# Seven-product units: partial sums kept in PSUM, two units interleaved, some GpSimd work given to VectorE

## The chip, the cores and the metric

The kernel runs on one core of one Trainium2 chip. The metric is the device time of one execution in microseconds. The core's engines run side by side, each through its own list of instructions in order: TensorE (PE; its weight loads are shown as PEld), VectorE (DVE), ScalarE (ACT), GpSimd (POOL), and SyncE (SP), whose queue issues all DMA transfers. The engines wait for each other through semaphores. Matrix products land in PSUM, eight banks of 512 fp32 per partition; GpSimd is not used on PSUM here. Everything else lies in SBUF or in DRAM.

## The reference

One layer of a hybrid backbone on 1024 latent tokens and 256 context tokens, D_MODEL = 1024, fp32:

```python
h   = modulate(rmsnorm(x, norm1_w), shift1, scale1)
z, f, uv, gate, ... = split(h @ w_in)            # IN_COLS columns, gate: 3 * 1024
m   = sigmoid(g0) * (y_ssd @ w_ssd_o) + sigmoid(g1) * (y_fft @ w_fft_o) + sigmoid(g2) * (y_gmlp @ w_gmlp_o)
x   = x + gate1 * (m @ w_out)
h2  = modulate(rmsnorm(x, norm2_w), shift2, scale2)
a, v = split(dwconv3(h2 @ ffn_w_up))             # 2 * 2816 columns, conv along rows of 64 tokens
x   = x + gate2 * ((silu(a) * v) @ ffn_w_down)
out = rmsnorm(x, final_norm_w)
```

y_ssd is a bidirectional state-space scan, y_fft a two-dimensional Fourier mixing, y_gmlp a spatial gating.

## The kernel before

Activations lie with channels on partitions and the 1024 tokens along the free axis, in tiles of 128 x 1024. Each fp32 factor is split in two parts (a high part rounded by ScalarE's copy, and the rest, a subtraction on VectorE or GpSimd), and each product is three matmuls: high x high, high x low, low x high.

The large products use a seven-product form on 2 x 2 blocks. A *unit* computes two output tiles of 128 channels (r = 0, 1) for two token halves of 512 (h = 0, 1): four quarters. With weight blocks A11, A12, A21, A22 the weights are A11 (1), A12 (2), S2 = A21 + A22 - A11 (6), S1 = A21 + A22 (5), S3 = A11 - A21 (7), A12 - S2 (3) and A22 (4); the activation operands B1 to B7 are built once per stage. With products P1 to P7 the quarters are

```
(0,0) = P1 + P2            (0,1) = P1 + P6 + P5 + P3
(1,0) = P1 + P6 + P7 + P4  (1,1) = P1 + P6 + P7 + P5
```

`unit_steps` (line 820) runs one unit. `raw` (824) loads the four weight blocks, `s_` (829) forms the sums on VectorE, `put` (834) splits a weight into a tile of `wpool` (6 buffers): the high part on ScalarE (836), the low part on GpSimd (837). `prod` (840) issues the matmuls of one product, 3 x kh (843 to 845). P1 + P2 goes to bank X, P6 + P7 + P4 to bank Y, P5 + P3 to bank Z; X and Y come from four rotating banks, Z from two. ScalarE copies P1 out of X (856). `add` (849) forms each of the other three quarters in SBUF tiles r0 and r1 from bank Y, the copy p1 and bank Z, in five VectorE additions per unit; then `consume` gets each quarter. Between P6 and P7, and between P7 and P4, Y has to be read by VectorE.

The stages with such units, in order:

- gates (`gate_unit`, 1050): 12 units, kh = 4. `consume` is a sigmoid on ScalarE into r0 or r1 (1052), stored to Sg. After each addition of most units a step of `modulation` (1066) runs on VectorE as side work: two products with a running sum, L1078.
- SSD merge (1113): 4 units, kh = 4. `consume` multiplies by the loaded gate on VectorE (1117). The operand is built by `build` (786), mostly on VectorE, while the last gate units run.
- up projection (`up_unit`, 1316): 22 units, kh = 4. `consume` is a convolution of width 3 over tokens: a ScalarE activation (1306) and two VectorE instructions (1308, 1310), all reading the quarter; for r = 0 a tanh (1328, ScalarE) and a VectorE product (1329); after each of (0,1) and (1,0) a GpSimd product with the gated half (1331). After every second unit four VectorE sums (1353 to 1356) form the operands of the down stage and are stored to Gd. The first two units start early, amid the second norm.
- down projection (1364): the inner dimension in chunks of 6, 6, 4 and 4 tiles (the last 2 tiles are done plainly). A chunk loads its operand parts from Gd and splits them (166, 167), then runs 4 units, kh = 3 or 2. `consume` adds the quarter, scaled by the gate g2, onto the tile xf in SBUF (1386). xf comes from Xs and takes the two buffers that the gate tiles gt of the up stage used.
- the fourth chunk by token halves (`unit_by_halves`, 931), with the last products and the final norm between its halves (1446).

The order of the instructions on each engine is made before the run by a planner that simulates the engines; `tc.high_priority` moves instructions ahead in it (PRE for the weights, CRIT for the additions).

```python
        prod(Y, 6, True)
        add(c12, Y, p1, True)
        prod(Z, 5, True)
        prod(Y, 7, False)
        add(c22, Y, p1, True)
        add(c22, Z, c22, True)
        consume(1, 1, c22, R)
```

Of the kernel before, what the change touches and what calls it, by code (L numbers as in the profile page):

```python
# [32 lines left out]
def hybrid_block_kernel(ctx: ExitStack, tc: tile.TileContext, a, dbg=None):  # L33
# [158 lines left out]
    # ------------------------------------------------ first norm and its modulation  # L192
# [100 lines left out]
    # dt and the decays that follow from it, tokens on partitions  # L293
# [45 lines left out]
    # ------------------------------------------------ step sizes; context pass for the initial states  # L339
# [66 lines left out]
    # ------------------------------------------------ xBC and the chunked scan  # L406
# [214 lines left out]
    # ------------------------------------------------ z gate, group norm, gMLP branch  # L621
# [57 lines left out]
    # ------------------------------------------------ Fourier branch: both transforms  # L679
# [43 lines left out]
    # ------------------------------------------------ gMLP branch  # L723
# [29 lines left out]
    # ------------------------------------------------ seven-product form of the large products  # L753
# [66 lines left out]
    def unit_steps(src0, src1, kh, B, consume, nm, side=None, early=None):  # L820
        n = kh * P
        w = {}
# [11 lines left out]
        def put(p, ap):  # L834
            t = wpool.tile([P, 2, n], F32R, tag="w", name=f"w{p}{nm}")
            S.activation(t[:, 0, :], ap, AF.Copy)  # L836
            G.tensor_tensor(t[:, 1, :], ap, f32(t)[:, 0, :], op=ALU.subtract)  # L837
            w[p] = t.rearrange("p q (k c) -> p q k c", c=P)

        def prod(o, p, first):  # L840
            for k in range(kh):
                xh, xl_ = B[p][k]
                PE.matmul(o, w[p][:, 0, k, :], xh, start=first and k == 0, stop=False, skip_group_check=not first)  # L843
                PE.matmul(o, w[p][:, 0, k, :], xl_, start=False, stop=False, skip_group_check=not first)
                PE.matmul(o, w[p][:, 1, k, :], xh, start=False, stop=k == kh - 1, skip_group_check=not first)

        def add(o, x, y, hook=False):
            with tc.high_priority(offset=CRIT):
                ins = V.tensor_tensor(o, x, y, op=ALU.add)  # L849
            if hook and side is not None:  # L850
                with tc.issue_after(ins.ins):
                    next(side, None)

        def copy_p1():
            with tc.high_priority(offset=CRIT):
                S.activation(p1, X, AF.Copy)
# [3 lines left out]
        if early:  # L860
            with tc.high_priority(offset=PRE):
                put(1, raw(11, 0, 0))
                put(2, raw(12, 0, 1))
            prod(X, 1, True)
            copy_p1()
            yield
            prod(X, 2, False)
            yield
            with tc.high_priority(offset=PRE):
                a11, a21 = raw(11, 0, 0), raw(21, 1, 0)  # L870
                a22, a12 = raw(22, 1, 1), raw(12, 0, 1)
                s1_ = s_(1, a21, a22, ALU.add)
                s2_ = s_(2, s1_, a11, ALU.subtract)
                put(3, s_(4, a12, s2_, ALU.subtract))
            W = ps_small("w" + nm, early[0])
            prod(W, 3, True)
            yield
            with tc.high_priority(offset=PRE):
                put(6, s2_)
                put(5, s1_)  # L880
                put(7, s_(3, a11, a21, ALU.subtract))
                put(4, a22)
            yield
        else:
            with tc.high_priority(offset=PRE):
                a11, a21 = raw(11, 0, 0), raw(21, 1, 0)
                a22, a12 = raw(22, 1, 1), raw(12, 0, 1)
                put(1, a11)
                s1_ = s_(1, a21, a22, ALU.add)
                s2_ = s_(2, s1_, a11, ALU.subtract)  # L890
                put(6, s2_)
                put(5, s1_)
                s3_ = s_(3, a11, a21, ALU.subtract)
                put(7, s3_)
                put(2, a12)
                s_(4, a12, s2_, ALU.subtract, s2_)
                put(3, s2_)
                put(4, a22)

        Y = ps4("Y" + nm)  # L900
        Z = ps_small("z" + nm, early[1] if early else ("c", "c2")[un[0] % 2])
        un[0] += 1
        r0 = tpool.tile([P, L], F32, tag="acc", name="r0" + nm)
        r1 = tpool.tile([P, L], F32, tag="acc", name="r1" + nm)
        R = (r0, r1)
        c12, c21, c22 = r0[:, HB:L], r1[:, 0:HB], r1[:, HB:L]
        if early:
            consume(0, 0, X, R)
        else:
            prod(X, 1, True)  # L910
            copy_p1()
        prod(Y, 6, True)
        add(c12, Y, p1, True)
        prod(Z, 5, True)
        prod(Y, 7, False)
        add(c22, Y, p1, True)
        add(c22, Z, c22, True)
        consume(1, 1, c22, R)
        if not early:
# [526 lines left out]
    for u in tail:  # L1446
        next(u)
# [116 lines left out]
```

## Time and profile before

| | |
|---|---|
| time, median of 3 runs | 1992.35 us (1987.56 to 1993.89) |
| profiled execution: span from first to last instruction | 1985.5 us |
| profiled execution: its own time | not listed; the runs lie 2 to 8 us above the span |
| TensorE busy | 1782.9 us, 90% of the span |
| VectorE busy | 1506.0 us, 76% |
| GpSimd busy | 1049.2 us, 53% |
| ScalarE busy | 821.3 us, 41% |

Times are in microseconds from the start of the span, mean durations in the view of groups of instructions in nanoseconds. A line of the profile names the source line, the engine, the operation and its tiles as out<-in (buffer numbers are left out: `up` in a name is the up stage, `g` the gates, `p` the SSD merge, `d` the down stage). Matmuls are pipelined: one is shown with about 0.39 us, but the next starts after about 0.23; so their spacing is read from the starts. A few matmul records may be missing. "idle before <- X" is the time for which an engine stood before an instruction, and what ended it. PEclk is the granted TensorE clock as a share of full speed.

### The profile page before, as it was taken

To read this page: it belongs to the slowest core of one execution; us is meant where nothing else is said; L and a number is where in the kernel's file an instruction comes from. 1 tells how busy PE (TensorE), PEld (TensorE's weight loads), DVE (VectorE), ACT (ScalarE), POOL (GpSimd) and SP (SyncE) were. 2 spreads that over 40 slices of the span, in tenths; PEclk is the share of its full clock that TensorE was granted. 3 is DMA by queue.
4 is the path that set the end of the run, shared out by engine and by line. 5 is a ranking of instruction groups with operands and counts; after the bars stand their busy time and mean duration, and the time that the engine had idled before them with its cause. 6 is when DMAs were issued, how large, how long until landed. Compare 5 with 4: busy or idle time off the path is not lost. (4 is left out here: it accounts for less than half of the span.)

```text
span 1985.5 us, 23581 instructions
## 1 busy us (share of the span) xinstructions
PE 1782.9 (90%) x8148; PEld 1414.7 (71%) x8148; DVE 1506.0 (76%) x1976; ACT 821.3 (41%) x1416; POOL 1049.2 (53%) x707
## 2 busy tenths in 40 slices
PE   4899989888997999998899998898989898889888
PEld 3688766666676888786677886676777776667667
DVE  6876576786676757878786458988888888978896
ACT  5444345554532433334232344343344344434433
POOL 3222265466444655554458555655555565755664
PEclk9999999999998999999999998899999999899998
DMA  8022446554542136662354631132222224643422
GB/s 319 11 67 75 141 151 169 143 171 128 159 142 83 66 110 217 218 218 90 106 182 162 225 132 58 70 105 80 85 85 96 80 85 145 219 145 120 149 88 85
DMA packets 139423, 257.21 MB, mean 130 GB/s; under 512 B 14876, under 2 KB 55708, under 8 KB 137896
## 3 DMA queue, kind: packets, MB, share of 16 engines
q1 hardware_dynamic: 139304, 255.71, 39.1%
q8 instruction: 64, 1.05, 0.2%
q14 instruction: 55, 0.45, 0.1%
HBM read 202.56 MB, written 53.10 MB: 129 GB/s over the span
## 5 line engine op out<-in xcount | busy, mean ns | idle before, releaser
L1078 DVE CUSTOM_DVE_ANT_0 ctanh<-ctanh,crow 128x512 f32<-128x512 f32 x64 | 71.7, 1139 | 24.6 <-DMA ctanh<-in_wmod_dram 24.4
L286 DVE SCALAR_TENSOR_TENSOR acc<-psx,convw,acc 128x1023 f32<-128x1023 f32 (+1 forms) x48 | 61.3, 1277 | 22.9 <-ACT acc L282 22.4
L1331 POOL TENSOR_TENSOR gt<-gt,aa 128x512 f32<-128x512 f32 x44 | 60.1, 1367 | 33.3 <-DVE gt L1310 26.6
L1126 POOL TENSOR_TENSOR pwo<-rwo,pwo 128x512 fp32r<-128x512 f32 x32 | 47.4, 1488 | 48.8 <-ACT pwo L1125 43.4
L555 DVE SCALAR_TENSOR_TENSOR rf<-rs,ncuml,rf 128x128 f32<-128x128 f32 x128 | 47.3, 416 | 31.5 <-ACT rf L554 29.1
L561 POOL TENSOR_TENSOR rf<-rf,G 128x512 f32<-128x512 f32 x32 | 46.0, 1441 | 45.0 <-DVE G L558 34.7
L843 PE MATMUL Yup<-bhh,w4up 128*128 128x512 f32 x88 | 40.9, 464 | 25.8 <-DVE r1up L849 25.8
L558 DVE SCALAR_TENSOR_TENSOR G<-cbm,dtl,G 128x128 f32<-128x128 f32 x128 | 58.6, 516 | 5.5 <-ACT G L557 5.5
L1328 ACT ACTIVATE ft<-aa 128x512 f32<-128x512 f32 x44 | 27.8, 631 | 82.9 <-DVE aa L1310 82.9
L1306 ACT ACTIVATE gt<-r1up,fconvb,fconvw 128x512 f32<-128x512 f32 x44 | 35.8, 814 | 54.2 <-DVE r1up L849 53.6
L837 POOL TENSOR_TENSOR w6up<-S2up,w6up 128x512 fp32r<-128x512 f32 x22 | 35.3, 1603 | 42.2 <-ACT w6up L836 42.2
L554 ACT ACTIVATE rf<-rf,ncuml 128x128 f32<-128x128 f32 x128 | 41.1, 390 | 31.5 <-DMA rf<-Rd 31.5
L1308 DVE SCALAR_TENSOR_TENSOR gt<-r1up,fconvw,gt 128x504 f32<-128x504 f32 x44 | 43.3, 985 | 9.9 <-ACT gt L1306 9.7
L837 POOL TENSOR_TENSOR w5up<-S1up,w5up 128x512 fp32r<-128x512 f32 x22 | 30.4, 1382 | 37.9 <-ACT w5up L836 34.2
L157 PE MATMUL pso<-mh,pwo 128*128 128x512 f32 x128 | 50.2, 392 | 0.0
L153 PE MATMUL pso<-mh,pwo 128*128 128x512 f32 x128 | 49.8, 390 | 0.0
L155 PE MATMUL pso<-ml,pwo 128*128 128x512 f32 x128 | 49.8, 389 | 0.0
L837 POOL TENSOR_TENSOR w2up<-A12up,w2up 128x512 fp32r<-128x512 f32 x22 | 32.1, 1459 | 33.5 <-ACT w2up L836 33.5
L1310 DVE SCALAR_TENSOR_TENSOR gt<-r1up,fconvw,gt 128x504 f32<-128x504 f32 x44 | 48.0, 1092 | 0.4
L510 DVE TENSOR_TENSOR scr<-po,ro 128x512 f32<-128x512 f32 x32 | 21.8, 683 | 34.9 <-ACT ro L497 34.6
L1329 DVE SCALAR_TENSOR_TENSOR aa<-ft,aa 128x512 f32<-128x512 f32 x44 | 46.1, 1047 | 2.7 <-ACT ft L1328 2.7
L520 PE MATMUL pS<-scr,Bt 128*128 128x512 f32 x56 | 32.5, 665 | 15.6 <-DVE scr L510 15.2
(1116 smaller groups left out, 6836.1 us busy)
## 6 DMA issues: line engine op xcount, KB each, us to landing
gr<-Gd SPq DMA_DIRECT2D x70, 256.0 KB, 4.5
ctanh<-in_wmod_dram SPq DMA_DIRECT2D x64, 256.0 KB, 3.1
Gd<-gt SPq DMA_DIRECT2D x10, 1536.0 KB, 6.1
wm<-in_wmod_dram SPq DMA_DIRECT2D x16, 512.0 KB, 9.8
ro<-Rd SPq DMA_DIRECT2D x64, 128.0 KB, 3.3
rf<-Rd SPq DMA_DIRECT2D x32, 256.0 KB, 4.7
rs<-Rd SPq DMA_DIRECT2D x32, 256.0 KB, 3.4
sg<-Sg SPq DMA_DIRECT2D x16, 512.0 KB, 3.6
```

The costliest lines, as they stand in the source:

```text
L153: PE.matmul(o, wh[:, k, :], xh[:, sl], start=st, stop=False)
L155: PE.matmul(o, wh[:, k, :], xl[:, sl], start=False, stop=False)
L157: last_op["mm"] = PE.matmul(o, wl[:, k, :], xh[:, sl], start=False, stop=sp)
L286: V.scalar_tensor_tensor(acc[:, lo:hi], ps[:, lo + o:hi + o], cw[:, t, j:j + 1], acc[:, lo:hi], op0=ALU.mult, op1=ALU.add)
L555: V.scalar_tensor_tensor(E[:, h, :], rs[:, h, :], ncum[:, c, 16 + f:17 + f], E[:, h, :], op0=ALU.add, op1=ALU.min)
L558: V.scalar_tensor_tensor(Gm[:, h, :], cbm[:, 1, :], dtl[:, c, 16 + f:17 + f], Gm[:, h, :], op0=ALU.mult, op1=ALU.add)
L837: G.tensor_tensor(t[:, 1, :], ap, f32(t)[:, 0, :], op=ALU.subtract)
L1078: V.tensor_tensor_reduce(out=wm[:, i], in0=wm[:, i], in1=cr[:, HS[i]], scale=0.5, scalar=0.0, op0=ALU.mult, op1=ALU.add, accum_out=mod2[:, ...
L1126: G.tensor_tensor(t[:, 1, :], raw, f32(t)[:, 0, :], op=ALU.subtract)
L1310: V.scalar_tensor_tensor(a3[:, :, 0:63], p3[:, :, 1:64], fcw[:, t, 2:3], a3[:, :, 0:63], op0=ALU.mult, op1=ALU.add)
L1329: V.scalar_tensor_tensor(ac, th, 1.0, ac, op0=ALU.add, op1=ALU.mult)
L1331: G.tensor_tensor(gt[:, 2 * q + h, :], gt[:, 2 * q + h, :], aa[:, HS[h]], op=ALU.mult)
```

## The change

- The partial sums stay in PSUM. P1, P6, P7 and P4 accumulate one after the other in bank Y, P5 and P3 in Z, P2 alone in X. ScalarE copies Y out after P1 (p1), after P6 (u2) and after P7 (u3). VectorE makes three additions per unit: X + p1 in place in PSUM, Z + u3 into SBUF, Z + u2 in place in PSUM. The quarter (1,0) is bank Y itself. So three of the four quarters reach `consume` in PSUM.
- Units are cut into three steps, and `run_units` interleaves two of them: the first product of the next unit (and the preparation of its weights) comes ahead of P4 and P3 of the current one.
- Gates: the sigmoid writes into p1, u2 or u3, and each half row is stored by itself.
- Up stage: the gate product (1331 before) and the low parts of weights 2 and 3 go from GpSimd to VectorE. The sums of a pair and their stores are issued after the last step of its second unit, that is behind the first product of the next unit.
- Down stage: `sum_steps` has no additions. After each product `consume` adds the bank as it stands onto xf, seven times per unit; the low parts of weights 3 and 4 go to VectorE. The token-half units do the same and their steps are staggered over the four units.
- The first two up units keep their order; their additions go to one tile U, the last one in place in PSUM.

The diff, cut to its core:

```diff
-            G.tensor_tensor(t[:, 1, :], ap, f32(t)[:, 0, :], op=ALU.subtract)
+            (V if p in on_v else G).tensor_tensor(t[:, 1, :], ap, f32(t)[:, 0, :], op=ALU.subtract)
...
+    def unit_steps(src0, src1, kh, B, consume, nm, side=None, on_v=()):
+        w = seven_weights(src0, src1, kh, nm, on_v)
...
+        prod(Y, w[1], B[1], kh, True)
+        keep(p1, Y)
+        yield
...
+        prod(Z, w[5], B[5], kh, True)
+        prod(Y, w[6], B[6], kh, False)
+        keep(u2, Y)
+        prod(X, w[2], B[2], kh, True)
+        add(X, X, p1)
+        consume(0, 0, X, p1)
+        prod(Y, w[7], B[7], kh, False)
+        keep(u3, Y)
+        add(u3, Z, u3)
+        consume(1, 1, u3, u3)
+        yield
+        prod(Y, w[4], B[4], kh, False)
+        consume(1, 0, Y, p1)
+        prod(Z, w[3], B[3], kh, False)
+        add(Z, Z, u2)
+        consume(0, 1, Z, u2)
+        yield
...
+    def sum_steps(src0, src1, kh, B, consume, nm, on_v=()):
...
+        prod(Y, w[1], B[1], kh, True)
+        out(0, 0, Y)
+        yield
...
+        prod(Z, w[5], B[5], kh, True)
+        out(1, 1, Z)
+        prod(Y, w[6], B[6], kh, False)
+        out(0, 1, Y)
+        prod(X, w[2], B[2], kh, True)
+        out(0, 0, X)
+        prod(Y, w[7], B[7], kh, False)
+        out(1, 1, Y)
+        yield
+        prod(Z, w[3], B[3], kh, False)
+        out(0, 1, Z)
+        prod(Y, w[4], B[4], kh, False)
+        out(1, 0, Y)
+        yield
+
+    def run_units(units):
+        units = iter(units)
+        cur = next(units)
+        next(cur)
+        while cur is not None:
+            next(cur)
+            nxt = next(units, None)
+            if nxt is not None:
+                next(nxt)
+            next(cur)
+            cur = nxt
...
-        def consume(r, h, src, R):
-            S.activation(R[r][:, HS[h]], src, AF.Sigmoid)
-            if r != h:
-                SY.dma_start(Sg[b][d + 4 * r], R[r])
+        def consume(r, h, src, spare):
+            S.activation(spare, src, AF.Sigmoid)
+            SY.dma_start(Sg[b][d + 4 * r][:, HS[h]], spare)
...
-                G.tensor_tensor(gt[:, 2 * q + h, :], gt[:, 2 * q + h, :], aa[:, HS[h]], op=ALU.mult)
+                V.tensor_tensor(gt[:, 2 * q + h, :], gt[:, 2 * q + h, :], aa[:, HS[h]], op=ALU.mult)
+        args = (a["wup"][j], a["wup"][NFF + j], 4, B2, consume, f"up{j}")
+        return early_steps(*args, early) if early else unit_steps(*args, on_v=(2, 3))
...
+            return (sum_by_halves if halves else sum_steps)(*args, on_v=(3, 4))
```

## Rows read from the trace of the kernel before

**Rows 1.** Busy times in four stretches: us, then each engine, PEclk, DMA share, GB/s.
```profile
753.28:890.45 137.17, 135.48 (x590) 109.53 (x588) 109.72 (x176) 48.16 (x85) 74.64 (x50) 1.00 0.65 217
890.45:1012.00 121.55, 105.71 (x433) 83.22 (x431) 91.70 (x101) 43.23 (x66) 57.37 (x37) 0.96 0.33 111
1315.32:1670.60 355.28, 323.38 (x1345) 254.75 (x1344) 297.43 (x337) 139.79 (x224) 205.32 (x144) 0.96 0.25 89
1716.00:1957.00 241.00, 214.97 (x886) 170.14 (x885) 206.21 (x252) 95.12 (x169) 148.44 (x122) 0.94 0.38 121
```
In each stretch the engines stand in the order PE, PEld, DVE, ACT, POOL.

**Rows 2.** TensorE's timeline: first matmul of a product and of the next.
```profile
1315.32 0.39 PE L843 MATMUL Xup<-bhh,w1up 128*128 128x512 f32 x1
...
1318.04 0.39 PE L843 MATMUL Yup<-bhh,w6up 128*128 128x512 f32 x1
```

**Rows 3.** Waits from 1250 to 1690 us: total, times, longest.
```profile
ACT aa L1306 <- POOL gt L1331: 57.5, 20, 4.0
...
PEld Yup L843 <- DVE r1up L849: 31.4, 18, 5.5
```

**Rows 4.** TensorE's timeline at its longest stop in the up stage.
```profile
1377.33 0.80 PE L843 MATMUL Yup<-bhh,w4up 128*128 128x512 f32 x1 [5.04 <-DVE r1up L849]
1377.92 0.63 PE L844 MATMUL Yup<-blh,w4up 128*128 128x512 f32 x1
1378.35 0.63 PE L845 MATMUL Yup<-bhh,w4up 128*128 128x512 f32 x1
```

**Rows 5.** Timeline of all engines: a VectorE and a GpSimd instruction that meet.
```profile
1411.44 1.67 POOL L837 TENSOR_TENSOR w7up<-S3up,w7up 128x512 fp32r<-128x512 f32 x1 [0.69 <-ACT w7up L836]
...
1411.99 1.66 DVE L1310 SCALAR_TENSOR_TENSOR aa<-r0up,fconvw,aa 128x504 f32<-128x504 f32 x1
```

**Rows 6.** Single lines (min/median/max ns), then groups of 1315.32 to 1670.60 us.
```profile
L849 DVE TENSOR_TENSOR r1up<-Yup,p1up x44: 672/680/691, 1249.8 to 1714.6; 128x512 f32<-128x512 f32 x44
...
L831 DVE TENSOR_TENSOR S2up<-S1up,A11up x22: 676/680/1785, 1190.7 to 1658.8; 128x512 f32<-128x512 f32 x22
...
L1310 DVE SCALAR_TENSOR_TENSOR gt<-r1up,fconvw,gt 128x504 f32<-128x504 f32 x33 | 35.0, 1059 | 0.3
L1308 DVE SCALAR_TENSOR_TENSOR gt<-r1up,fconvw,gt 128x504 f32<-128x504 f32 x32 | 31.8, 995 | 7.2 <-ACT gt L1306 7.1
...
L831 DVE TENSOR_TENSOR S2up<-A12up,S2up 128x512 f32<-128x512 f32 x16 | 19.7, 1232 | 4.7 <-POOL w6up L837 4.7
L1310 DVE SCALAR_TENSOR_TENSOR aa<-r0up,fconvw,aa 128x504 f32<-128x504 f32 x16 | 19.1, 1193 | 0.3
...
L831 DVE TENSOR_TENSOR S1up<-A21up,A22up 128x512 f32<-128x512 f32 x16 | 16.1, 1008 | 0.0
...
L1308 DVE SCALAR_TENSOR_TENSOR aa<-Xup,fconvw,aa 128x504 f32<-128x504 f32 x16 | 11.7, 734 | 0.5
...
L1331 POOL TENSOR_TENSOR gt<-gt,aa 128x512 f32<-128x512 f32 x32 | 41.2, 1288 | 25.4 <-DVE gt L1310 22.9 <-DVE aa L1329 2.5
...
L856 ACT ACTIVATE p1up<-Xup 128x512 f32<-128x512 f32 x16 | 9.2, 578 | 0.0
```

**Rows 7.** TensorE's timeline near the gates' end; a wait of 680 to 915 us.
```profile
911.66 0.80 PE L843 MATMUL Yg<-hh,w4g 128*128 128x512 f32 x1 [5.72 <-DVE r1g L849]
...
ACT r0g L1052 <- DMA Sg<-r1g: 9.0, 5, 4.3
```

**Rows 8.** Down stage: groups of 1716 to 1957 us, then two timeline rows.
```profile
L1386 DVE SCALAR_TENSOR_TENSOR xf<-r1d,g,xf 128x512 f32<-128x512 f32 x24 | 27.7, 1157 | 2.7 <-DMA xf<-Xs 2.3
...
L1386 DVE SCALAR_TENSOR_TENSOR xf<-Xd,g,xf 128x512 f32<-128x512 f32 x16 | 11.8, 740 | 1.2 <-PE Xd L845 1.2
...
L831 DVE TENSOR_TENSOR S1d<-A21d,A22d 128x384 f32<-128x384 f32 (+1 forms) x10 | 6.7, 670 | 0.0
...
1715.85 0.39 PE L843 MATMUL zd<-gh,w5d 128*128 128x512 f32 x1
...
1743.86 1.28 DVE L1386 SCALAR_TENSOR_TENSOR xf<-r1d,g,xf 128x512 f32<-128x512 f32 x1 [2.28 <-DMA xf<-Xs]
```

More of the change, by code (lines that the diff above doesn't have):

```diff
@@ L836, in put @@
             S.activation(t[:, 0, :], ap, AF.Copy)
-            G.tensor_tensor(t[:, 1, :], ap, f32(t)[:, 0, :], op=ALU.subtract)
[L838 to L845, printed above, removed]
@@ L847, in add, with prod @@
-        def add(o, x, y, hook=False):
+            (V if p in on_v else G).tensor_tensor(t[:, 1, :], ap, f32(t)[:, 0, :], op=ALU.subtract)
+            return t.rearrange("p q (k c) -> p q k c", c=P)
+        return raw, s_, put
+    def prod(o, w, Bp, kh, first):
+        for k in range(kh):
+            xh, xl_ = Bp[k]
+            PE.matmul(o, w[:, 0, k, :], xh, start=first and k == 0, stop=False, skip_group_check=not first)
+            PE.matmul(o, w[:, 0, k, :], xl_, start=False, stop=False, skip_group_check=not first)
+            last_op["PE2"] = PE.matmul(o, w[:, 1, k, :], xh, start=False, stop=k == kh - 1,
+                                       skip_group_check=not first)
@@ L848, in add, with keep @@
+    def unit_steps(src0, src1, kh, B, consume, nm, side=None, on_v=()):
+        w = seven_weights(src0, src1, kh, nm, on_v)
+        def keep(dst, ps):
+            with tc.high_priority(offset=CRIT):
+                S.activation(dst, ps, AF.Copy)
+        def add(o, x, y):
             with tc.high_priority(offset=CRIT):
                 ins = V.tensor_tensor(o, x, y, op=ALU.add)
-            if hook and side is not None:
+            if side is not None:
                 with tc.issue_after(ins.ins):
@@ L900, in unit_steps @@
[L900 to L913, printed above, removed]
@@ L1000, in unit_by_halves @@
         un[0] += 1
[L1001 to L1004 removed]
+        prod(Z, w5, B[5], kh, True)
+        out(1, 1, Z)
         yield
[L1007 to L1009 removed]
+        prod(Z, w3, B[3], kh, False)
+        out(0, 1, Z)
+        yield
     Bh = {p: [] for p in ORDER}
@@ L1358, in hybrid_block_kernel, with gate_tile, up_stage, with_sums @@
         SY.dma_start(Gd[jp][:, 2:8, :], gt[:, 2:8, :])
+    def gate_tile(jp):
+        gts[jp] = mpool.tile([P, 8, HB], F32, tag="m", name=f"gt{jp}")
+    gate_tile(0)
+    for u in pre:
+        for _ in u:
+            pass
+    gate_sums(0)
+    def up_stage():
+        for j in range(2, NFF):
+            if j % 2 == 0:
+                gate_tile(j // 2)
+            yield up_unit(j)
+    def with_sums(units):
+        for j, u in enumerate(units, 2):
+            def steps(j=j, u=u):
+                for n_, _ in enumerate(u):
+                    if n_ == 2 and j % 2:
+                        gate_sums(j // 2)
+                    yield
+            yield steps()
+    run_units(with_sums(up_stage()))
     WHERE = {1: 0, 6: 5, 5: 4, 7: 6, 2: 2, 3: 3, 4: 7}
     j0 = 0
-    tail = []
     for ci, kc in enumerate(FF_CHUNKS[:-1]):
@@ L1381, in hybrid_block_kernel, with down_unit, consume @@
                 SY.dma_start(xlv(d, t=xf), Xs[d])
-        for d in range(4):
-            def consume(r, h, src, R=None, d=d):
+        def down_unit(d, halves):
+            def consume(r, h, src):
                 dd = d + 4 * r
@@ L1444, in last_out, with staggered @@
                              xf[k // 4][:, k % 4 - 1:k % 4 + 1, hs])
-    for u in tail:
-        next(u)
+    def staggered(n):
+        for i in range(n + len(tail) - 1):
+            for q in range(n):
+                if 0 <= i - q < len(tail):
+                    next(tail[i - q])
+    staggered(3)
     last_products(0)
     last_norm(0)
-    for u in tail:
-        next(u)
+    staggered(2)
     last_out(0)
```

260 lines of the change are left out of this document (123 added, 137 removed).

## The prediction

> **What bounds the kernel now.** I read the busy times in stretches first, cut at the first matmul of a unit, because the change touches four stages that have different limits. The gate stretch, the first row of [rows 1], holds seven units in 137.17 us, 19.60 us each. The up stretch (third row) holds sixteen in 355.28 us, 22.21 us each. Each of these units issues 84 matmuls. The matmul timeline gives their price: twelve take 1318.04 - 1315.32 = 2.72 us [rows 2], 0.227 us each, so 84 need 19.05 us. The gate stretch is thus within 0.55 us of what TensorE can do; the up stretch loses 3.16 us in every unit.
>
> The table of waits says on what [rows 3]: TensorE's weight loads stood 31.4 us before the fourth product of Y, always for the VectorE addition that takes Y out of its bank. The timeline shows the worst one [rows 4]: 5.04 us of idleness at 1377.33 us, after which the matmuls start 0.43 us apart (1377.92 to 1378.35) and not 0.227. [...]
>
> Why is the addition late? VectorE is busy 297.43 of 355.28 us, 84%, 18.6 us per unit. It is in order, and its instructions with two SBUF inputs are long where GpSimd is at work: at 1411.99 us one took 1.66 us, until GpSimd's weight split (1411.44, 1.67 us) had ended and half a microsecond more; that is the pair in [rows 5]. The second weight sum takes 676 ns at its shortest and 1785 at its longest, while the 44 additions from PSUM all lie between 672 and 691 ns [rows 6]. So each GpSimd instruction can cost VectorE time, and an instruction with a PSUM source is immune.
>
> **The change, part by part: up stage, 20 units.** *Removed from VectorE:* two of five additions, 0.68 us each [rows 6], -1.4 us per unit. *Moved to a PSUM source:* the convolutions of the two off-diagonal quarters. Such a pair costs 1.06 + 1.00 us from the SBUF sum r1 and 1.19 + 1.12 from r0 (of r0 one row is shown; its twin has 1119 ns), but 2 x 0.73 from Xup: -(2.06 - 1.46) - (2.31 - 1.46) = -1.45 us. *Added to VectorE:* two gate products and two splits, each a two-input SBUF instruction: between 0.68 (uncollided) and 1.01 us (the weight sum S1, a middle one; S2 from A12 has 1.23), 2.7 to 4.1 us; I take 3.4, since fewer GpSimd instructions are left to collide with. *Relief:* GpSimd has 9 instructions per unit now (seven splits, two products of 1.29 us [rows 6]) and 5 after. S1 stands 0.33 us above the uncollided price; the ten two-input instructions that stay (four weight sums, two convolutions, two after the tanh, two gate sums) carry some 3.4 us of this, and 4/9 of it, 1.5 us, goes. VectorE: 18.6 - 1.4 - 1.45 + 3.4 - 1.5 = **17.6 us** per unit; without any relief and at the high price 19.9.
>
> So TensorE's 19.05 us becomes the larger demand, if its waits go. They change their kind: between P6 and P7, and between P7 and P4, Y must be copied out by ScalarE (0.58 us, as the copy of X today), with one product (2.72 us) of another bank in between; VectorE is waited for only at P3, two products behind P7. ScalarE is busy 139.79 of 355.28 us, 39%, and gets two copies of 0.58 us per unit more: hidden. An addition that also writes to PSUM is not in the trace; its bounds are 0.67 us, the shortest with an SBUF target, and twice 0.68, as if reading and writing followed each other (1.4 us more per unit); I take 0.68, the row of the same length and source. The gate sums move behind the next unit's first product; they queue ahead of additions as today, but no longer wait for GpSimd (57.5 us of ScalarE's waits are for that product too [rows 3]). Their two stores move with them on the sync queue, behind weight loads of the next unit; nothing reads them before the down stage and gt has two buffers, so I cost this at nothing; without that cover, the loads behind them would come late by a landing, some 6 us per pair.
>
> The period: the gate stage, with VectorE at 109.72/137.17 = 80%, stays 0.55 us above the floor. Here VectorE would be at 17.6/20 = 88%, so more: 20.0 us. Gain (22.2 - 20.0) x 20 = **44 us**. Ends: 2.6 x 20 = 52 us at the gates' own distance; on the other side the second rival.
>
> [...]
>
> **Gate stage, 10 interleaved units:** from 19.60 to about 19.2 us: **4 us**, between 0 and 5.5. Each unit stores four half rows in place of two whole ones, so the sync queue gets 24 issues more and weight loads queue behind stores; and the second sigmoid into p1 must wait for the store of the first. ScalarE waited 9.0 us for such stores already [rows 7]. Covered by the unit's 19 us of matmuls, and by weights split some products ahead: 0, at worst twice the 9.0 us, -18.
>
> **Gates to SSD merge (890 to 1012 us):** about 433 matmuls in 121.55 us [rows 1], some 98 us of work. At 911.66 us TensorE stood 5.72 us for the addition r1g, while VectorE split the next stage's operand, and then started at the low clock (0.80 us) [rows 7]. A ScalarE copy takes its place: **5 us**, between 0 and 10, since the operand must still be built by VectorE.
>
> **Down stage and token halves (1716 to 1957):** 886 matmuls at 0.227 are 201 of 241 us. In each of 12 units VectorE loses five additions (3.4 us) and gets seven accumulations from PSUM at 0.74 us in place of one at 0.74 and three at about 1.16 [rows 8]: 7.6 to 5.2 us. Two weight splits come, at the 0.67 us of a weight sum there 1.3 us. Net -1.1 us, 13 us in all; the four units by token halves lose three additions, gain one accumulation and two splits, about nothing. VectorE is 206.21 of 241 us busy, 86%, and its collisions fall too, so I count **12 us** of this as time. A new wait stands against it: today partial results lie in SBUF when xf is late (VectorE stood 2.28 us at 1743.86 us [rows 8]); now every bank waits for xf at once, and the operand splits queue behind it on VectorE. The up stage's matmuls end at 1715.85 us, 28 us before that landing, and TensorE spends much of these on stops for the operand splits; if the splits still cover the landing, 0; if not, at worst a third of the 28 us, 10 us, once. Ends for the stage: -10 to 30.
>
> **Sum:** 44 + 4 + 5 + 12 = 65 us. The profiled execution spans 1985.5 us, 6.85 below the median of the runs, 1992.35; nothing ahead of 680 us or around the span changes, so I take the sum from the median: **1927 us**.
>
> **Rivals.** *ScalarE's queue takes the wait over.* Its copies that free Y stand in order behind activations that read what VectorE has just added; if VectorE runs late, these block the copies and TensorE stops as before. For it: ScalarE waits long for others in the up stage already. Against: it is 39% busy. Half the stage's loss would stay: period 21.3, 18 us, with 10 us from the rest: 1964 us.
>
> *VectorE becomes the bound: slower.* If the four added instructions collide as the worst today and no relief comes, it needs 19.9 us per unit, and at today's share of 84% the period is 23.7 us: +1.5 x 20 = +30 us, 2022 us. It decides as soon as its busy time per unit passes 18.7 us. Against: collisions need GpSimd, which has four instructions less.
>
> *The waits are others' anyway.* Where the weights or the operands come just as late as the additions, the planner's order only shifts the stop: 1990 us. For it: operand splits bound the chunk starts of the down stage; against: in the up stage the addition is by far TensorE's longest wait.
>
> **How the numbers follow.** Forecast 0.62, ScalarE 0.22, no effect 0.07, slower 0.09. A measurement of this kernel tells about 0.3%, 6 us, from no change. Faster 0.84, same 0.07, slower 0.09. At its best ends the forecast gains 52 + 5.5 + 10 + 30 = 97 us, 1895; with 44 us and the bad ends of the rest (-18, 0, -10) 16, 1976, but these fall together hardly ever. The range is 1893 to 1970, which holds the ScalarE case too and leaves out the last two.
>
> **What would show it.** In the changed profile: up units 20 us apart, the clock at 1.00 there, no wait of TensorE for a VectorE addition before P4, two convolution pairs more at 0.73 us, VectorE near 17.6 us per unit and GpSimd near 7. Wrong if TensorE waits for ScalarE's copies for more than 1 us per unit, if VectorE is over 95% busy in the up stage, or if the first down unit stops for xf.

## The result, and the profile after

The changed kernel takes 1909.99 us (median of 4 runs, 1908.35 to 1914.46) against 1989.95 us for the kernel before, measured beside it. The ratio is 0.9615, with a 95% interval of 0.9583 to 0.9647: 80 us faster, where 65 were forecast, and inside the range. Three of the forecast's four terms came out otherwise than written, though, and two of the errors cancelled in part.

The page of the changed kernel begins so (engine, busy us, share of the span, instructions):

```profile
span 1908.4 us, 23564 instructions
## 1 busy us (share of the span) xinstructions
PE 1753.8 (92%) x8148; PEld 1412.3 (74%) x8148; DVE 1411.5 (74%) x1988; ACT 852.3 (45%) x1472; POOL 876.9 (46%) x591
```

The span is 77.1 us shorter than the 1985.5 us of before. Where the 77.1 us went is read from four marks that both traces have: the first gate matmul into zg, the last matmuls of the SSD merge (into zp) and of the up stage (into zup), and the end. The groups of TensorE instructions on these banks show the first mark as the first start in zg's row, the second and the third as the last start in zp's and zup's (the columns are shortest, median and longest ns, then first and last start). The changed kernel, then the kernel before:

```profile
L844 PE MATMUL zg<-tx,w5g x48: 389/389/389, 681.3 to 896.9; 128*128 128x512 f32 x48
...
L846 PE MATMUL zp<-bhy,w3p x16: 389/389/389, 970.5 to 1025.3; 128*128 128x512 f32 x16
...
L846 PE MATMUL zup<-bhh,w3up x80: 389/389/395, 1285.4 to 1647.6; 128*128 128x512 f32 x80
```

```profile
L843 PE MATMUL zg<-tx,w5g x48: 387/389/798, 680.4 to 899.3; 128*128 128x512 f32 x48
...
L845 PE MATMUL zp<-bhy,w3p x16: 388/389/393, 961.8 to 1021.6; 128*128 128x512 f32 x16
...
L845 PE MATMUL zup<-bhh,w3up x80: 388/389/398, 1294.0 to 1715.6; 128*128 128x512 f32 x80
```

The differences between marks:

| stretch | before | after | gain | forecast |
|---|---|---|---|---|
| start to first gate matmul | 680.4 | 681.3 | -0.9 | 0 |
| gates and SSD merge | 341.2 | 344.0 | -2.8 | 4 + 5 |
| from there to the end of the up stage | 694.0 | 622.3 | 71.7 | 44 |
| down stage to the end | 269.9 | 260.8 | 9.1 | 12 |

So the up stage gave 28 us more than its term, and the gates with the SSD merge took 12 us that had been counted as gain. The stretches show both (columns as in [rows 1]: PE, PEld, DVE, ACT, POOL, granted clock, DMA share, GB/s):

```profile
753.00:890.00 137.00, 137.00 (x606) 113.48 (x605) 80.53 (x139) 57.81 (x101) 72.90 (x51) 1.00 0.64 200
890.00:1025.00 135.00, 112.02 (x472) 89.35 (x471) 95.18 (x135) 53.54 (x87) 52.70 (x38) 0.91 0.43 136
1320.00:1620.00 300.00, 300.00 (x1325) 248.47 (x1325) 260.80 (x362) 152.43 (x251) 113.65 (x79) 1.00 0.31 104
```

In 300 us of the up stage TensorE is busy without a gap, with 1325 matmuls; at 84 per unit that is 15.77 units, 19.02 us each. The same 300 us of the kernel before read:

```profile
1320.00:1620.00 300.00, 273.44 (x1137) 214.43 (x1136) 250.35 (x286) 118.22 (x190) 173.52 (x122) 0.97 0.26 90
```

1137 matmuls are 13.54 units, 22.16 us each. 3.14 us in each of 20 units are 63 of the 71.7 us; the other 9 lie at the start of the up stage, where the two early units run: from zup's first matmul to its first matmul with w3up it takes 63.2 us (1221.7 to 1284.9) in place of 75.8 (1217.7 to 1293.5), of which some 3 us are counted in the 20 units already. The table of TensorE's waits in these 300 us is empty (between 1250 and 1650 us two remain, of 1.7 and 1.0 us), and with the waits of [rows 3] the low clock is gone: PEclk is 1.00 throughout, where the kernel before has 0.97 in the mean and 0.50 behind its stops (911.66 to 914.39 and 1377.33 to 1381.00 us). The gates reach the same pace, 606 matmuls in 137 us or 19.0 us per unit, against 19.60 in [rows 1].

The groups of VectorE in the same 300 us show what became of each price in [rows 6] (count, busy us, mean ns):

```profile
L1372 DVE TENSOR_TENSOR gt<-gt,aa 128x512 f32<-128x512 f32 x31 | 28.9, 932 | 0.0
L1370 DVE SCALAR_TENSOR_TENSOR aa<-ft,aa 128x512 f32<-128x512 f32 x32 | 27.3, 854 | 1.3 <-ACT ft L1369 1.3
L1351 DVE SCALAR_TENSOR_TENSOR gt<-Uup,fconvw,gt 128x504 f32<-128x504 f32 x16 | 19.1, 1192 | 0.3
L1349 DVE SCALAR_TENSOR_TENSOR gt<-Uup,fconvw,gt 128x504 f32<-128x504 f32 x16 | 15.2, 952 | 0.0
L830 DVE TENSOR_TENSOR S1up<-A21up,A22up 128x512 f32<-128x512 f32 x15 | 14.2, 948 | 14.8 <-DMA A22up<-in_wup_dram 14.3 <-issue 0.5
L830 DVE TENSOR_TENSOR S2up<-S1up,A11up 128x512 f32<-128x512 f32 x16 | 12.0, 750 | 0.0
L1349 DVE SCALAR_TENSOR_TENSOR aa<-zup,fconvw,aa 128x504 f32<-128x504 f32 x16 | 11.8, 737 | 0.3 <-ACT aa L1347 0.3
L1349 DVE SCALAR_TENSOR_TENSOR gt<-Yup,fconvw,gt 128x504 f32<-128x504 f32 x16 | 11.8, 736 | 0.0
...
L1351 DVE SCALAR_TENSOR_TENSOR gt<-Yup,fconvw,gt 128x504 f32<-128x504 f32 x16 | 11.7, 733 | 0.0
...
L836 DVE TENSOR_TENSOR w3up<-S2up,w3up 128x512 fp32r<-128x512 f32 x16 | 11.0, 686 | 22.1 <-ACT w3up L835 22.1
...
L876 DVE TENSOR_TENSOR zup<-zup,Uup 128x512 f32<-128x512 f32 x16 | 11.0, 684 | 0.0
...
L830 DVE TENSOR_TENSOR S2up<-A12up,S2up 128x512 f32<-128x512 f32 x16 | 10.9, 679 | 0.0
L830 DVE TENSOR_TENSOR S3up<-A11up,A21up 128x512 f32<-128x512 f32 x16 | 10.8, 677 | 0.0
L836 DVE TENSOR_TENSOR w2up<-A12up,w2up 128x512 fp32r<-128x512 f32 x15 | 10.2, 678 | 0.0
L876 DVE TENSOR_TENSOR Uup<-zup,Uup 128x512 f32<-128x512 f32 x15 | 10.1, 676 | 0.0
```

The four weight sums in the same 300 us of the kernel before:

```profile
L831 DVE TENSOR_TENSOR S2up<-A12up,S2up 128x512 f32<-128x512 f32 x13 | 16.6, 1274 | 3.5 <-POOL w6up L837 3.5
...
L831 DVE TENSOR_TENSOR S1up<-A21up,A22up 128x512 f32<-128x512 f32 x14 | 13.7, 976 | 0.0
L831 DVE TENSOR_TENSOR S3up<-A11up,A21up 128x512 f32<-128x512 f32 x13 | 12.3, 946 | 0.0
L831 DVE TENSOR_TENSOR S2up<-S1up,A11up 128x512 f32<-128x512 f32 x14 | 11.6, 831 | 0.0
```

The two convolutions of a quarter in PSUM cost 0.74 us each; an addition in place in PSUM 0.684, one into SBUF 0.676. S2 from A12 fell from 1274 ns to 679. Per unit VectorE is busy 260.80 / 15.77 = 16.5 us (17.6 were forecast), GpSimd 113.65 / 15.77 = 7.2.

**The stretch that lost.** Between 890 and 1025 us TensorE is busy for 112.02 of 135 us at a mean clock of 0.91. TensorE's timeline of the changed kernel has one long stop there (the next longest is 1.9 us):

```profile
935.56 0.80 PE L844 MATMUL zp<-bhy,w5p 128*128 128x512 f32 x1 [17.35 <-ACT bhy L166]
```

bhy is the high part of the SSD merge's operand, split from T2y, which `build` makes on VectorE. T2y's first instruction starts at 932.3 us in the changed kernel and at 896.9 us in the kernel before. T1y and T2y live in the buffers (tags tmp and zz) that the modulation's tiles hold till it ends; T1y starts at 930.81 us, 0.2 us after the modulation's last instruction. The modulation's line in the changed kernel, then in the kernel before:

```profile
L1117 DVE CUSTOM_DVE_ANT_0 ctanh<-ctanh,crow x64: 675/693/1796, 743.9 to 930.0; 128x512 f32<-128x512 f32 x64
```

```profile
L1078 DVE CUSTOM_DVE_ANT_0 ctanh<-ctanh,crow x64: 677/1092/1822, 743.1 to 893.5; 128x512 f32<-128x512 f32 x64
```

The last one starts 36.5 us later after the change, although each is shorter in the median. A step of the modulation is handed out after an addition: in the kernel before after four of a unit's five (not after each, as its description above says; the one without `True` hands out none), now after three. 32 steps at four per unit are done in 8 units; at three, the 10 units that hand them out give 30, and two remain for after the gates.

### The profile page after: what moved, and what is told of

Read it like the earlier page. It is cut to its first block, busy times and chain, and to the rows that moved or that the text cites. A ratio compares the mean times of both kernels' runs of the same rounds, so it can differ in the third digit from the quotient of the medians.

```text
span 1908.4 us, 23564 instructions
## 1 busy us (share of the span) xinstructions
PE 1753.8 (92%) x8148; PEld 1412.3 (74%) x8148; DVE 1411.5 (74%) x1988; ACT 852.3 (45%) x1472; POOL 876.9 (46%) x591
## 5 line engine op out<-in xcount | busy, mean ns | idle before, releaser
L1117 DVE CUSTOM_DVE_ANT_0 ctanh<-ctanh,crow 128x512 f32<-128x512 f32 x64 | 57.7, 918 | 24.6 <-DMA ctanh<-in_wmod_dram 24.5
L836 POOL TENSOR_TENSOR w1up<-A11up,w1up 128x512 fp32r<-128x512 f32 x22 | 29.4, 1334 | 97.2 <-ACT w1up L835 88.0
L836 POOL TENSOR_TENSOR w7up<-S3up,w7up 128x512 fp32r<-128x512 f32 x22 | 31.6, 1436 | 89.1 <-ACT w7up L835 49.5
L1450 DVE SCALAR_TENSOR_TENSOR xf<-Yd,g,xf 128x512 f32<-128x512 f32 x64 | 47.1, 742 | 12.1 <-PE Yd L846 11.8
L836 POOL TENSOR_TENSOR w4up<-A22up,w4up 128x512 fp32r<-128x512 f32 x22 | 34.8, 1580 | 23.4 <-ACT w4up L835 23.4
L497 ACT ACTIVATE ro<-ro 128x512 f32<-128x512 f32 x32 | 20.1, 628 | 55.7 <-DMA ro<-Rd 50.5
L557 ACT ACTIVATE G<-cbm,dtl 128x128 f32<-128x128 f32 x128 | 39.6, 388 | 6.5 <-DVE cbm L545 6.5
L166 ACT ACTIVATE gh<-gr 128x1024 fp32r<-128x1024 f32 (+1 forms) x36 | 36.5, 1032 | 12.7 <-DMA gr<-Gd 6.8
L844 PE MATMUL Yup<-bhh,w7up 128*128 128x512 f32 x88 | 35.3, 401 | 6.4 <-DVE Uup L956 6.4
```

Source lines behind the costliest of these rows:

```text
L836: (V if p in on_v else G).tensor_tensor(t[:, 1, :], ap, f32(t)[:, 0, :], op=ALU.subtract)
L1117: V.tensor_tensor_reduce(out=wm[:, i], in0=wm[:, i], in1=cr[:, HS[i]], scale=0.5, scalar=0.0, op0=ALU.mult, op1=ALU.add, accum_out=mod2[:, ...
L1450: V.scalar_tensor_tensor(xv, src, g2[:, dd:dd + 1], xv, op0=ALU.mult, op1=ALU.add)
```

## Experiments

The question for the up stage was whether the partial sums in PSUM or the work moved off GpSimd made its gain, and whether the interleaving did; for the SSD merge, whether the pacing made its loss.

**The sums in PSUM alone, the moves alone.** First the changed kernel with all low parts and the gate product back on GpSimd, then the kernel before with only those moved:

```diff
-            (V if p in on_v else G).tensor_tensor(t[:, 1, :], ap, f32(t)[:, 0, :], op=ALU.subtract)
+            G.tensor_tensor(t[:, 1, :], ap, f32(t)[:, 0, :], op=ALU.subtract)
...
-                V.tensor_tensor(gt[:, 2 * q + h, :], gt[:, 2 * q + h, :], aa[:, HS[h]], op=ALU.mult)
+                G.tensor_tensor(gt[:, 2 * q + h, :], gt[:, 2 * q + h, :], aa[:, HS[h]], op=ALU.mult)
```

> The changed kernel with the gate product and all weight splits back on GpSimd. Theory (keeping the sums in PSUM and interleaving removed TensorE's waits; the move of work to VectorE is minor): the up unit stays below 19.6 us and the time within 12 us of the changed kernel, 1910 to 1922 us. Rival (the move off GpSimd is what freed VectorE of collisions): up units of 20.5 us or more, 1940 us or more.

Measured: 1943.81 us, ratio 0.9754 (0.9710 to 0.9797).

```diff
-            G.tensor_tensor(t[:, 1, :], ap, f32(t)[:, 0, :], op=ALU.subtract)
+            (V if p in on_v else G).tensor_tensor(t[:, 1, :], ap, f32(t)[:, 0, :], op=ALU.subtract)
...
-                G.tensor_tensor(gt[:, 2 * q + h, :], gt[:, 2 * q + h, :], aa[:, HS[h]], op=ALU.mult)
+                V.tensor_tensor(gt[:, 2 * q + h, :], gt[:, 2 * q + h, :], aa[:, HS[h]], op=ALU.mult)
```

> The kernel before with only the moves: gate product on VectorE, low parts of weights 2 and 3 (up stage) and 3 and 4 (down stage) on VectorE. Theory (the moves are minor, the waits for additions stay): 1975 to 2005 us, up units within 1 us of 22.2. Rival (the moves are the larger part of the gain): below 1960 us, up units of 20.5 us or less.

Measured: 1943.19 us, ratio 0.9778 (0.9739 to 0.9817). Each half alone is worth about 47 us of 80 (by the ratios 49 and 44), so the moves are no minor part; both theories fell, and both rivals' numbers came. From the SSD merge's last matmul to the up stage's the two take 659.6 us (1027.9 to 1687.5) and 657.6 us (1016.0 to 1673.6): gains of 34.4 and 36.4 us where both together gain 71.7. The same 300 us, of the sums in PSUM alone, then of the moves alone:

```profile
1320.00:1620.00 300.00, 285.83 (x1229) 228.25 (x1228) 252.05 (x279) 138.42 (x233) 180.77 (x133) 1.00 0.27 95
```

```profile
1320.00:1620.00 300.00, 289.50 (x1244) 229.99 (x1242) 281.93 (x369) 126.38 (x207) 109.08 (x74) 1.00 0.28 98
```

These are 20.50 and 20.26 us per unit: gains of 1.66 and 1.90 us on 22.16. Together they would make 3.56 us; 3.14 came, which is the whole loss: at the 0.227 us of [rows 2] 84 matmuls take 19.05 us, and the changed kernel's unit takes 19.02. What TensorE's weight loads and ScalarE still wait for with the sums in PSUM alone, between 1320 and 1620 us (total, times, longest):

```profile
PEld Yup L844 <- ACT Uup L872: 15.3, 14, 1.5
...
PEld Yup L846 <- POOL w1up L836: 7.2, 7, 1.1
```

```profile
ACT aa L1347 <- DVE zup L876: 39.5, 15, 3.3
...
ACT aa L1347 <- POOL gt L1372: 12.0, 6, 2.0
```

That is the prediction's first rival: TensorE waits for ScalarE's copies of Y, and ScalarE stands in activations that need VectorE's additions and GpSimd's product. The second row is a wait that the prediction didn't have for this case: the low part of weight 1 comes late from GpSimd, which makes all seven again. In the changed kernel the same activations wait 9.2 us for zup in place of 39.5, and no longer for GpSimd; ScalarE still stands 37.2 us for the gate product, now VectorE's, but no copy of Y comes late by it. With the moves alone the old wait stays, smaller (16.0 us in all for r1up, the longest 1.7 us, in place of 22.8 and 5.5).

**The moves one by one,** in the kernel before: the gate product alone, and the two weight splits alone (each a part of the edit above).

> The kernel before with the gate product alone on VectorE; all splits stay on GpSimd. Theory (VectorE stood idle for GpSimd's product ahead of the sums of a pair, and additions queued behind these sums): most of the up stage's gain of the moves, up units of 20.3 to 21.3 us instead of 22.3, 1950 to 1970 us, and VectorE's waits for the product, 40 us in the up stage, gone. Rival (what counts is fewer GpSimd instructions to collide with, whichever they are): half of it, as two of the four moved instructions per unit, and no more than the splits alone give: 1965 us or more, equal to the splits alone.

Measured: 1971.66 us, ratio 0.9920 (0.9892 to 0.9948).

> The kernel before with the two splits per unit alone on VectorE (weights 2 and 3 up, 3 and 4 down); the gate product stays on GpSimd. Theory of the product: little, up units of 21.7 us or more, 1975 us or more apart from some 8 us of the down stage. Rival (collisions): half of the moves' gain, up units of about 21.3 us, 1967 us.

Measured: 1963.45 us, ratio 0.9888 (0.9864 to 0.9912). The gains are 13 and 22 us against 47 together (by the ratios 16, 22 and 44), so the theory of the product fell, and both times are near the rivals'. In the up stage the paces are 300 x 84 / 1167 = 21.59 us and 300 x 84 / 1191 = 21.16 us. Whether the pair is worth more than its parts stays open: from the SSD merge's last matmul to the up stage's the gains are 8.6 and 13.3 us against 36.4, but that is one profile each, and by the ratios 38 against 44 lies within their intervals.

The rivals' reason, fewer meetings of the two engines, holds for the splits only. A sum over the timelines of these 300 us shows it: the time by which VectorE's instructions with two SBUF inputs exceed 0.68 us (0.73 for a convolution) is 5.0 us per unit in the kernel before, 5.5 with the product alone, 4.1 with the splits alone, 3.3 with both moves, 4.8 with the sums in PSUM alone and 2.1 in the changed kernel. With the product alone VectorE collides more, not less, and is busy 278.24 us of these 300 or 20.0 us per unit, itself more than TensorE's 19.05. What it no longer has is the wait for GpSimd's product ahead of the gate sums (17.1 and 14.0 us in the kernel before). That this wait makes its gain is not shown by itself.

**The interleaving undone.** `run_units` of the changed kernel runs each unit to its end before the next:

```diff
-        units = iter(units)
-        cur = next(units)
...
+        for u in units:
+            for _ in u:
+                pass
```

> The changed kernel with the units run one after the other instead of interleaved; all else as changed. Theory (each copy of Y needs a product of another bank behind it, and without the next unit's first product P4 waits for the copy after P7): 1 to 1.5 us more per unit in 38 units, 1940 to 1965 us. Rival (the accumulation in PSUM alone does it, the planner fills the gap with other products): within 10 us of the changed kernel, below 1920 us.

Measured: 1910.98 us, ratio 0.9607 (0.9581 to 0.9634): no difference. The stretch of the up stage again has 1325 matmuls in 300 us. My theory fell: the planner puts the next unit's first product ahead of P4 and P3 by itself, in either form (in this run the next unit's P1 starts at 1406.28 us, P4 at 1416.70 and P3 at 1419.42; in the changed kernel at 1406.87, 1417.98 and 1420.70). VectorE's row is of use here:

```profile
1320.00:1620.00 300.00, 300.00 (x1325) 248.42 (x1324) 277.94 (x362) 151.24 (x252) 107.82 (x79) 1.00 0.30 104
```

VectorE is busy 277.94 us, 93% or 17.6 us per unit, and TensorE doesn't stand for a moment. With the sums in PSUM alone VectorE had less to do, 252.05 / 14.63 = 17.2 us per unit, and 1.45 us per unit were lost.

**The copies of Y on VectorE.** In the changed kernel `keep` copies out of PSUM on VectorE:

```diff
-                S.activation(dst, ps, AF.Copy)
+                V.tensor_copy(dst, ps)
```

> The changed kernel with the three copies of Y per unit on VectorE instead of ScalarE. Theory (TensorE has to be freed by an engine with slack; VectorE's busy time rises from 17 to about 18.9 us per unit and its queue comes between P6 and P7 again): up units of 20 us or more, the time 1925 to 1950 us. Rival (the total work is what counts, and 18.9 us still fits under TensorE's 19.05): up units below 19.4 us, within 8 us of the changed kernel.

Measured: 1939.47 us, ratio 0.9767 (0.9740 to 0.9795), 29 us slower than the changed kernel.

```profile
1320.00:1620.00 300.00, 291.79 (x1261) 237.43 (x1259) 291.20 (x392) 122.04 (x195) 109.51 (x76) 0.99 0.28 101
```

VectorE is at 97%, a unit takes 19.98 us, and TensorE waits for VectorE again (6.4 us for Uup, the longest 2.9). But two things changed at once: VectorE's work is 291.20 / 15.01 = 19.4 us per unit, not 18.9, and so more than TensorE's 19.05 by itself. The rival's condition didn't hold, and the run doesn't tell the late copies from the sheer amount of work. It shows that the copies don't fit on VectorE; on ScalarE, busy 51% in the changed kernel, they do.

**The pacing of the modulation.** The changed kernel with two steps at a unit's last addition, four per unit as before:

```diff
-                    next(side, None)
+                    for _ in range(steps):
+                        next(side, None)
...
-        add(Z, Z, u2)
+        add(Z, Z, u2, 2)
```

> The changed kernel, but the third addition of a gate unit is followed by two steps of the modulation, so that a unit carries four steps as in the kernel before (the change had left three additions, and so three steps). Theory (the modulation ends late and holds the buffers that the SSD merge's operand is built in): the last modulation product moves from 930 us to about 895 us, the 17.3 us for which TensorE waits at the start of the SSD merge go, and the time falls by 12 to 20 us, to about 1895 us. Rival (VectorE's own work on the operand is the bound there, wherever the modulation ends): within 4 us of the changed kernel, 1910 us.

Measured: 1899.11 us (1892.15 to 1903.98), ratio 0.9548 (0.9513 to 0.9583), 11 us less than the changed kernel (13 by the ratios). The modulation and the operand's row of this run:

```profile
L1118 DVE CUSTOM_DVE_ANT_0 ctanh<-ctanh,crow x64: 672/692/1772, 746.8 to 902.7; 128x512 f32<-128x512 f32 x64
...
L797 DVE TENSOR_TENSOR T2y<-yacc,T1y x2: 1210/1212/1214, 907.8 to 920.8; 128x1024 f32<-128x1024 f32 x2
```

The stop of 17.35 us is gone; the longest wait for the operand is now 1.7 us. The merge's last matmul starts at 1014.6 us, 332.2 us after the gates' first (682.4): 9.0 us less than before the change; the forecast had 4 + 5.

The counter-test takes one of the four steps from the kernel before:

```diff
-            add(c21, Y, p1, True)
+            add(c21, Y, p1)
```

> The kernel before with the step of the modulation behind each gate unit's fourth addition left out, so that a unit carries three as in the changed kernel. Theory (pacing of the modulation by the additions): its last product moves from 893 us to about 930 us, and the stretch from the first gate product to the end of the SSD merge grows from 341 us by 10 to 20 us: 2000 to 2010 us. Rival (the changed kernel's wait at the SSD merge has another cause): within 5 us of the kernel before.

Measured: 2004.57 us, ratio 1.0080 (1.0054 to 1.0107), some 16 us slower by the ratio. In its profile the modulation's last product starts at 939.7 us, the stretch of gates and merge takes 359.2 us (680.4 to 1039.6), 18.0 more than in the kernel before, and TensorE's weight loads wait for bhy:

```profile
PEld Yp L843 <- ACT bhy L166: 13.4, 2, 12.5
```

Nothing else was changed, so the pacing by itself makes a loss of that size.

**Further with it.** The same version with the modulation handed out one unit earlier, and the same version with the down stage's splits back on GpSimd:

```diff
-    run_units(gate_unit(b, d, md if (b, d) > (0, 1) else None) for b in range(3) for d in range(4))
+    run_units(gate_unit(b, d, md if (b, d) > (0, 0) else None) for b in range(3) for d in range(4))
```

> The version with two modulation steps at each unit's last addition (its last modulation product starts at 902.7 us), and the modulation handed out from the second gate unit on instead of the third. Theory (the operand build of the SSD merge waits for the modulation's buffers, and everything that brings its end forward by a unit pays): last modulation product near 883 us, operand T1y at its place, gates and SSD merge 3 to 8 us shorter than in that version, time 1886 to 1896. Rival (once the operand comes before its matmuls need it, nothing is left to gain; TensorE waits under 2 us for it in that version): same time as that version, 1893 to 1904, with VectorE's work only moved.

Measured: 1898.61 us, ratio 0.9561 (0.9524 to 0.9598). The last product of the modulation starts at 890.6 us, 12 us earlier, and the stretch of gates and merge takes 334.1 us (332.2 without): the rival was right; once the operand comes in time, nothing is left in its date.

```diff
-            return (sum_by_halves if halves else sum_steps)(*args, on_v=(3, 4))
+            return (sum_by_halves if halves else sum_steps)(*args)
```

> The version with two modulation steps at each unit's last addition, and the weight splits of the down stage all on GpSimd as in the kernel before. Theory (VectorE has slack in the down stage, and TensorE's stops there are for operand splits that VectorE makes, so two more weight splits per unit delay those): the down stage 2 to 4 us shorter than in that version, time 1889 to 1898. Rival (the moved splits pay there as in the up stage, about 1 us per unit over 16 units): 10 to 20 us longer, 1908 to 1920.

Measured: 1893.34 us (1888.46 to 1896.18), ratio 0.9535 (0.9502 to 0.9568). The rival is out. The theory's time came, but not in its place: from the up stage's last matmul to the end this run takes 1894.2 - 1636.3 = 257.9 us, the version with on_v 1893.2 - 1635.2 = 258.0. So in the down stage the two moved splits make no difference that these profiles show, and the intervals of the two versions overlap. Both beat the kernel before and the changed kernel; which of them is faster stays open. Their stretch of gates and merge differs by 5.6 us (332.2 and 337.8) with the same code there, so a difference of that size in one profile is not read as an effect. By the same measure the 2.9 us between the down stage's 9.1 and its 12 say little.

## Why the prediction was right, and where it was wrong

- **What bounds the up stage: right.** TensorE's wait for VectorE to empty Y and its low clock were the larger part of the loss, and both went. Between 1320 and 1620 us the weight loads of the kernel before waited 22.8 us for r1up, 1.7 of the 3.14 us per unit. A mean clock of 0.97 between 1.00 and 0.50 puts 18 of these 300 us at 0.50; at a spacing of 0.43 us for 0.227 [rows 4] about half of them is lost, an estimate of 0.7 us per unit. No wait for VectorE comes before P4, the clock is 1.00, two more convolution pairs are at 0.74 us, as forecast. None of the prediction's signs of being wrong came.
- **The up term, 44 us: direction right, size wrong, 71.7 us.** The step that failed is "Here VectorE would be at 17.6/20 = 88%, so more: 20.0 us": it took the distance to TensorE's floor from VectorE's share. The runs show that neither the share nor the work per unit sets it. At 87% (16.5 us per unit) and at 93% (17.6 us, the interleaving undone) nothing is lost; the sums in PSUM alone lose 1.45 us at 84% (17.2 us). The kernel before lost 3.1 us at 83% (18.5 us), the moves alone 1.2 us at 94% (19.0 us). Where time is lost, the tables of waits have TensorE waiting for a copy or an addition that frees Y; that this link sets the loss is what they suggest, not what one run isolates. The better end of the term, 52 us, was at the gates' distance of 0.55 us from the floor, some 3.8 us in the seven units; 1.7 us of these are TensorE's waits for VectorE's additions, and the distance went too. 63 us in 20 units where 44 were forecast are 19 of the missing 28 us; the other 9 lie at the start of the stage, which was not costed.
- **VectorE's demand, 17.6 us: 16.5.** The added instructions were sized well: two products at 0.932 and two splits at 0.678 and 0.686 are 3.23 us, where 3.4 were taken. The addition in place in PSUM was 0.684 us, as taken from the row into SBUF. The relief was undersized, 2.0 us in place of 1.5: the four weight sums fell from 976 + 831 + 1274 + 946 to 948 + 750 + 679 + 677 ns, 0.97 us, the two products after the tanh from 1092 to 854 ns each, 0.48 us, and the four gate sums of a pair of units by 0.68 us per unit; the two convolutions that stayed on SBUF got none (1041 + 975 before, 1192 + 952 ns after). The rest of the difference isn't traced to terms.
- **ScalarE's queue, the first rival:** it didn't come, but it was near: the sums in PSUM without the moves show it at work, at 20.50 us per unit. Its price didn't follow from its words: half of the 3.16 us lost leaves a period of 20.6 us and a gain of 32 us, not 21.3 and 18.
- **Gates, 4 us: right in its stage** (19.0 us per unit where 19.2 were taken; ScalarE waits for no store, so the bound of -18 didn't come in).
- **Gates to SSD merge, 5 us: wrong.** The step that failed is "a ScalarE copy takes its place: 5 us, between 0 and 10, since the operand must still be built by VectorE". The copy did take the place of that wait. But the start of T2y moved by 35 us, because the diff dropped one of four additions to which steps of the modulation were hooked, and those steps hold the operand's buffers. The text of the step had no way from an addition to a buffer; the diff had it (`add(c21, Y, p1, True)` on the side of before). With the pacing restored, the stretch of gates and merge gains 9.0 us on the kernel before in that version, and 7.1 and 3.4 us (334.1 and 337.8 against 341.2) in the two made from it, where 9 were forecast. That the sum of all terms lies within 15 us of the result owes something to luck: this loss hid 12 of the 28 us by which the up term was short.
- **Down stage, 12 us: 9.1.** The accumulations did become cheap, 0.74 us each, and the cover of xf's landing held: VectorE stood 1.32 us for xf once (before 1684.95 us), and no stop of TensorE follows from it. TensorE waits for accumulations elsewhere, 0.94 us before 1679.68 us, but that one had waited for its own product (2.90 us for Yd), not for xf. The stops for the operand splits stayed, 3.66 and 4.24 us for gl at 1653.87 and 1659.54 us. The term took VectorE's net relief in this stage for time; the last experiment puts two splits per unit back on GpSimd, and the time of the stage doesn't move (257.9 against 258.0 us).
- **A PSUM source against an SBUF source:** the prediction's means, 0.73 us from PSUM against 1.06 + 1.00 and 1.19 + 1.12 for a pair from SBUF [rows 6], compare an instruction without collisions with one that has them; so do 0.74 and 0.95 or 1.19 here. The shortest of each kind in the changed kernel is the fair pair, and these are alike, 724 ns from the SBUF tile Uup and 727 from the bank Yup:

```profile
L1349 DVE SCALAR_TENSOR_TENSOR gt<-Uup,fconvw,gt x22: 724/737/1384, 1258.0 to 1646.6; 128x504 f32<-128x504 f32 x22
L1349 DVE SCALAR_TENSOR_TENSOR gt<-Yup,fconvw,gt x22: 727/732/744, 1267.5 to 1655.6; 128x504 f32<-128x504 f32 x22
```

## What to carry to other kernels

How full an engine is doesn't say how late it is: here nothing was lost with VectorE at 93%, and 1.45 us per unit with it at 84%. Look for whom TensorE needs between two products, give that link to an engine with time (here ScalarE, busy 51%), and shorten what that engine's queue waits for ahead of it; here either half alone got about half of the up stage's gain (34.4 and 36.4 of 71.7 us). Before an instruction is removed, look at what is hooked to it: work paced by it comes later (here 36.5 us), and with it whatever waits for that work's buffers (TensorE, 17.35 us). The sum of durations is not a demand where instructions overlap, 0.68 us each with starts 0.60 us apart in the rows below; take starts.

## What the runs showed of the hardware

Two stretches of the changed kernel's timelines, VectorE's and then GpSimd's, show the meetings of the two engines at their simplest (start, us, engine):

```profile
1407.92 1.71 DVE L830 TENSOR_TENSOR S1up<-A21up,A22up 128x512 f32<-128x512 f32 x1 [1.79 <-DMA A22up<-in_wup_dram]
...
1410.15 0.68 DVE L876 TENSOR_TENSOR Xup<-Xup,p1up 128x512 f32<-128x512 f32 x1
1410.75 0.68 DVE L1372 TENSOR_TENSOR gt<-gt,aa 128x512 f32<-128x512 f32 x1
1411.35 0.68 DVE L830 TENSOR_TENSOR S2up<-A12up,S2up 128x512 f32<-128x512 f32 x1
...
1416.51 0.74 DVE L1349 SCALAR_TENSOR_TENSOR gt<-Uup,fconvw,gt 128x504 f32<-128x504 f32 x1
1417.28 1.65 DVE L1351 SCALAR_TENSOR_TENSOR gt<-Uup,fconvw,gt 128x504 f32<-128x504 f32 x1
...
1424.74 1.43 DVE L1372 TENSOR_TENSOR gt<-gt,aa 128x512 f32<-128x512 f32 x1
1426.10 0.73 DVE L1349 SCALAR_TENSOR_TENSOR aa<-zup,fconvw,aa 128x504 f32<-128x504 f32 x1
```

```profile
1407.78 1.29 POOL L836 TENSOR_TENSOR w6up<-S2up,w6up 128x512 fp32r<-128x512 f32 x1 [0.92 <-ACT w6up L835]
1413.89 1.30 POOL L836 TENSOR_TENSOR w7up<-S3up,w7up 128x512 fp32r<-128x512 f32 x1 [4.82 <-issue]
1416.58 1.81 POOL L836 TENSOR_TENSOR w4up<-A22up,w4up 128x512 fp32r<-128x512 f32 x1 [1.40 <-ACT w4up L835]
...
1425.58 1.75 POOL L836 TENSOR_TENSOR w5up<-S1up,w5up 128x512 fp32r<-128x512 f32 x1
```

The sum S1 that starts at 1407.92 us, inside a GpSimd split, ends at 1409.63, 0.56 us after the split (1409.07); the convolution at 1417.28 ends at 1418.93, 0.54 us after the split that ran to 1418.39. Started while GpSimd rests, the same kinds of instruction take 0.68 to 0.74 us. The convolution at 1426.10 us has a PSUM source; it takes 0.73 us in the middle of a split that runs to 1427.33. So in these rows a VectorE instruction with two SBUF inputs that starts inside a split lasts till the split has ended and half a microsecond more. All 53 of these that start inside a split between 1320 and 1620 us end 0.40 to 0.56 us after it, while the 50 with a PSUM source that do so take 0.67 to 0.74 us. In these 300 us GpSimd pays only where it comes second: the split at 1407.78, which met S1, took 1.29 us as at rest (1.30 at 1413.89), and none of the 25 splits that meet only later starters takes more than 1.30; but those at 1416.58 and 1425.58, which start while such a VectorE instruction runs (1416.51 and 1424.74), took 1.81 and 1.75.

Instructions of VectorE in a row start 0.60 us apart (1410.15, 1410.75, 1411.35) while each is shown with 0.68 us. The prediction added durations, which overstates what an instruction without a collision takes of VectorE by 0.08 us.
